# Two FFN blocks share one PSUM group for their down products, and VectorE makes all weight combinations and low parts

## The chip, the cores and the metric

One core of a Trainium2 chip. The time is device microseconds of one execution of the program. Before the change three runs took 2386.94, 2387.88 and 2385.5 us; their median is 2386.94 us. The profiled execution took 2381.64 us, of which its trace spans 2379.8.

## The reference, cut to what matters

Two layers; each mixes tokens and then runs a SwiGLU feed-forward network (FFN) on 1024 tokens of width 1024, with a hidden width of 2816 (22 blocks of 128). The change touches the FFN alone:

```python
h = modulate(rms_norm(x, g_ffn[l]), sh2, sc2)
f = (jax.nn.silu(h @ w_ffn_gate[l]) * (h @ w_ffn_up[l])) @ w_ffn_down[l]
x = x + gt2[:, None, :] * f
```

All of it is fp32. The layer's six modulation vectors come from `mod = c_act @ w_ada[l] + b_ada[l]`; those of the second layer are computed, as a side job, while the first layer's FFN runs.

## The kernel before

**Products in three parts.** A fp32 operand is split in two: a high part (rounded to fp32r, made by ScalarE) and a low part (the rest, a subtraction). A product is then three matmuls, high*high, high*low, low*high (`mm3`). "Low part" below means that subtraction.

**Blocks and jobs.** The FFN runs over 22 blocks f of 128 hidden columns. Blocks 0 and 1 are done first, in the plain way (`e_job`: 16 jobs of 12 matmuls). For f = 2 to 21 the gate and up products are made by a scheme that needs seven half-size products in place of eight: seven jobs a block (`p_job`, in the order 1, 5, 6, 2, 7, 3, 4), each of 12 matmuls into one of PSUM banks 4 to 7. Four of the seven take a sum or difference of weight halves (`comb`: q = u1 + u2, q = q - g1, u1 = g1 - u1, q = g2 - q). Then each job's weights are split: the high part on ScalarE (L1339), the low part on VectorE or GpSimd by the table `LO_ENG` (L1340). Before the change GpSimd makes all combinations (L1324) and three of seven low parts. A job's weights are prepared three jobs ahead (`look = 3`, four slots in the ring `PR`); the raw weights of the next block are loaded (`raw_load`, L1259) once job 4 has split the last of this block's.

**After a job.** `after` (L1360) adds the banks up on VectorE: seven additions out of PSUM a block, two multiplications, two SiLU on ScalarE. The block's result a (128 hidden columns x 1024 tokens) is split by `a_split` into the tile `A`: its right half after job 3, its left half after job 4, the block's last.

**Down products.** A block's down product has eight output pieces m. For each, `down_pair` does two groups (one for each half of the tokens) of three matmuls into two of PSUM banks 0 to 3, and one VectorE instruction of 128x1024 (`stt`, L204) adds the pair, times a gate, to x. They are put between the jobs by `hook`, which is called after each half job (six matmuls), 14 times a block: during block f, hooks 2 to 6 and 8 to 10 (`PAIRS`) carry the down pairs of block f - 1. So block f - 1's `A` is needed 18 matmuls after that block's last job. The down weights come through one raw buffer in halves (`dw_load`, `dw_split`) into the tile `DW`.

**Order.** TensorE runs the matmuls exactly in the order written. The other engines' orders are set by a scheduler when the program is built; each engine then works through its own list and stops at the first instruction whose operands aren't there. During the first layer's FFN `half_steps` (L1474) adds one piece of the second layer's modulation per half step: a 256 KB load, then one VectorE reduction (L1482).

**Ends.** The last two blocks' down products (20 and 21) stand in `down_tail` after the loop.

Of the kernel before, what the change touches and what calls it, by code (L numbers as in the profile page):

```python
# [17 lines left out]
HALF = 512  # L18
# [57 lines left out]
FIRST = 2  # L76
LO_ENG = {1: 0, 5: 1, 6: 0, 2: 1, 7: 0, 3: 1, 4: 0}
P_ORDER = (1, 5, 6, 2, 7, 3, 4)
PAIRS = {2: 0, 3: 1, 4: 2, 5: 3, 6: 4, 8: 5, 9: 6, 10: 7}
LATE = 11  # L80
# [51 lines left out]
class Trunk:  # L132
# [21 lines left out]

    def open(self, name, **tiles):
        cm = self.tc.tile_pool(name=name, bufs=1)
        pool = cm.__enter__()
        for nm, (n, dt) in tiles.items():
            setattr(self, nm, pool.tile([P, n], dt, name=f"{name}_{nm}"))
        return cm  # L160
# [1001 lines left out]
    def w_out(self, l):  # L1162
# [9 lines left out]
        self.hp = self.open(f"hx{l}", HX=(12 * U, F32R))  # L1172
        self.pp = self.open(f"prep{l}", FA2=(4 * U, F32))
        self.ap = self.open(f"kept{l}", FA1=(4 * U, F32))
# [125 lines left out]
    def e_hook(self, l, i):  # L1300
        if i == 0:
            self.dw_load(l, 0, 0)
        elif i == 2:
            self.shut(self.ap)
            self.ap = self.open(f"ffa{l}", A=(2 * U, F32R), DW=(2 * U, F32R))
            self.dw_split(0, 0)
            self.dw_load(l, 0, 1)
        elif i == 3:
            for half in range(2):
                self.e_split(0, half)  # L1310
            self.free.append(self.ea[0, 0])
        if i >= 4:
            self.down_pair(l, 0, i - 4)
        if i == 4:
            self.dw_split(0, 1)
            self.dw_load(l, 1, 0)
        elif i == 7:
            self.dw_split(1, 0)
            self.dw_load(l, 1, 1)

    def p_job(self, l, f, p):
        nc = self.nc
        g1, g2, u1, u2, q = [self.f(o, HALF) for o in (8 * U, 8 * U + HALF, 9 * U, 9 * U + HALF, 14 * U + HALF)]
        comb = lambda out, a, b, op=ALU.subtract: nc.gpsimd.tensor_tensor(out=out, in0=a, in1=b, op=op)  # L1324
        operand = {1: 0, 2: 1, 5: 2, 6: 3, 7: 4, 3: 5, 4: 6}[p]

        def load():
            o = self.PR()
            src = {1: g1, 5: q, 6: q, 2: g2, 7: u1, 3: q, 4: u2}[p]
            if p == 5:  # L1330
                comb(q, u1, u2, ALU.add)
            elif p == 6:
                comb(q, q, g1)
            elif p == 7:
                comb(u1, g1, u1)
            elif p == 3:
                comb(q, g2, q)
            hi, lo = self.RA[:, o:o + HALF], self.RA[:, o + HALF:o + U]
            self.act(hi, src, AF.Copy)  # L1339
            (nc.gpsimd if LO_ENG[p] else nc.vector).tensor_tensor(out=lo, in0=src, in1=hi.bitcast(F32),  # L1340
                                                                  op=ALU.subtract)
            if p == 4 and f + 1 < NRUN:
                self.raw_load(l, f + 1, "wg", 8 * U)
                self.raw_load(l, f + 1, "wu", 9 * U)
            return hi, lo
# [55 lines left out]
    def ad(self, f):  # L1401
        return (self.HX[:, :2 * U], self.HX[:, 2 * U:4 * U]) if f == NRUN - 1 else (self.A[:, :], self.DW[:, :])

# [18 lines left out]
    def down_pair(self, l, f, m):  # L1422
        d = self.fd()
        for j, n in enumerate(NS):
            self.down(f, m, n, self.bank(d + j), True, True)
        x = self.f(self.X0 + m * U, U).rearrange("p (a b) -> p a b", a=2)
        self.stt(x, self.PS[:, d:d + 2, :], self.f(self.mod[l] + 40 + m, 1), x, ALU.mult, ALU.add)

    def hook(self, l, f):
# [4 lines left out]
        if f == FIRST:  # L1434
            if i < 4:
                self.down_pair(l, 0, 4 + i)
            if i == 3:
                self.dw_split(1, 1)
                for half in range(2):
                    self.e_split(1, half)  # L1440
                self.free.append(self.ea[1, 0])
                self.dw_load(l, f, 0)
            m = i - 4
            prev = 1
        else:
            m = PAIRS.get(i, -1)
            prev = f - 1
            if i == 0:
                self.dw_load(l, f, 0)
        if f == NRUN - 1:  # L1450
            if i == 4:
                self.dw_split(f, 0)
                self.dw_load(l, f, 1)
            elif i == 6:
                self.dw_split(f, 1)
            return
        if 0 <= m < 8:
            self.down_pair(l, prev, m)
            if m == 3:
                self.dw_split(f, 0)  # L1460
                self.dw_load(l, f, 1)
            if m == 7:
                self.dw_split(f, 1)
        if self.late and i >= LATE:
            self.late()
            self.late = None
# [49 lines left out]
    def ffn(self, l, nb):  # L1516
# [29 lines left out]
        if not end:  # L1546
            ts = [self.fp(8 + k) for k in range(8)]
            na = self.norm(l + 1, 0, A, banks[0], ts, TUNE["ht_a"])
# [172 lines left out]
```

## Time and profile before

| | |
|---|---|
| runs | 2386.94, 2387.88, 2385.5 us |
| profiled execution | 2381.64 us |
| span of its trace | 2379.8 us |
| TensorE (PE) busy | 2235.3 us, 94% |
| weight loads (PEld) busy | 1793.7 us |
| VectorE (DVE) busy | 1863.8 us, 78% |
| ScalarE (ACT) busy | 967.1 us, 41% |
| GpSimd (POOL) busy | 765.8 us, 32% |

The FFN is the better part of the span: the first layer's lies at about 510 to 1200 us, the second's at 1670 to 2340 us. In a row of a timeline the first number is the start, the second how long the row lasts, and a bracket at the end says how long the engine was idle before it and what ended the idleness. Rows of several equal instructions are merged (xN). Starts of consecutive instructions on one engine can be closer than the length of one, since an instruction's end overlaps the next one's start. TensorE's matmuls have modelled ends, so the idle time of its weight loads (PEld, one for each matmul) tells more of its waits than that of the matmuls.

### The profile page before, as it was taken

How to read it: one execution, taken by the hardware profiler on the slowest of the kernel's cores; microseconds unless marked ns; L12 is line 12 of the kernel's file. 1: busy time of each engine (PE TensorE's matmuls, PEld its weight loads, DVE VectorE, ACT ScalarE, POOL GpSimd, SP SyncE). 2: the span in 40 equal slices, each digit the busy share in tenths (PEclk: the TensorE clock that was granted, in tenths of full speed). 3: DMA queues.
4: the chain of work that ended last, by engine and by line, in shares of the span. 5: the costliest groups of instructions: out<-in, count | busy, mean ns of one | idle time of the engine just before them, and what ended most of it. 6: DMA issues, size and time to landing. Idle time of an engine off the chain costs nothing.

```text
span 2379.8 us, 27251 instructions
## 1 busy us (share of the span) xinstructions
PE 2235.3 (94%) x9802; PEld 1793.7 (75%) x9802; DVE 1863.8 (78%) x2709; ACT 967.1 (41%) x1598; POOL 765.8 (32%) x559
## 2 busy tenths in 40 slices
PE   6987998999999999999989989899999999999996
PEld 4765876777777777788867777678778888888885
DVE  8888788788888888887775676987877777777775
ACT  5375475543222222222344746745422222222234
POOL 4224366202233333333200325740123323333333
PEclk9997999989999999999999999999999999999998
DMA  7323423321333333321221132323011111111112
GB/s 294 101 69 110 138 76 120 121 94 40 97 111 111 111 103 114 107 80 54 80 98 57 40 110 66 110 75 115 27 58 54 54 53 49 49 50 53 54 49 71
DMA packets 77422, 203.81 MB, mean 86 GB/s; under 512 B 8931, under 2 KB 13027, under 8 KB 77286
## 3 DMA queue, kind: packets, MB, share of 16 engines
q1 hardware_dynamic: 73540, 183.41, 23.7%
q10 hardware_dynamic: 3746, 18.66, 2.3%
q8 instruction: 77, 1.26, 0.2%
q14 instruction: 59, 0.48, 0.1%
HBM read 193.64 MB, written 8.39 MB: 85 GB/s over the span
## 4 chain that ended last, share of the span: by engine, by line
PE 72%; DVE 17%; issue 4%; ACT 4%; POOL 2%; DMA 2%; SPq 0%; POOLq 0%; ACTq 0%; DVEq 0%
PE psum L190 72%; DVE rounded L201 3%; DVE plain L201 2%; DVE plain L204 1%; DVE ffa_A L201 1%; DVE psum L885 1%; ACT rounded L198 1%; DMA plain<-in_ada 1%; ACT plain L198 1%; ACT lru_LF L198 1%; DVE psum L201 1%; DVE prep_FA L204 1%; DVE plain L312 1%; ACT ffa_A L198 1%; POOL plain L1582 1%
## 5 line engine op out<-in xcount | busy, mean ns | idle before, releaser
L190 PE MATMUL psum<-rounded 128*128 128x512 f32 (+2 forms) x4332 | 1055.4, 392 | 28.9 <-DVE rounded L201 10.2
L190 PEld LDWEIGHTS psum<-rounded 128*128 128x128 f32 (+1 forms) x4332 | 814.3, 190 | 204.3 <-DVE rounded L201 14.1
L204 DVE SCALAR_TENSOR_TENSOR plain<-psum,plain 128x1024 f32<-128x1024 f32 (+2 forms) x416 | 474.4, 1147 | 198.3 <-PE psum L190 195.8
L198 ACT ACTIVATE rounded<-plain 128x512 fp32r<-128x512 f32 (+4 forms) x412 | 272.5, 666 | 736.5 <-PE psum L190 643.3
L190 PE MATMUL psum<-ffa_A,ffa_DW 128*128 128x512 f32 (+1 forms) x2040 | 526.3, 392 | 15.6 <-DVE ffa_A L201 6.9
L190 PEld LDWEIGHTS psum<-ffa_A,ffa_DW 128*128 128x128 f32 x2040 | 379.0, 189 | 112.1 <-DVE ffa_A L201 16.3
L1324 POOL TENSOR_TENSOR plain<-plain 128x512 f32<-128x512 f32 x160 | 224.3, 1402 | 740.3 <-DMA plain<-in_wu 355.9
L190 PE MATMUL psum<-hx_HX,rounded 128*128 128x512 f32 x1488 | 381.6, 393 | 0.0
L190 PEld LDWEIGHTS psum<-hx_HX,rounded 128*128 128x128 f32 x1488 | 279.7, 188 | 61.7
L1340 POOL TENSOR_TENSOR rounded<-plain,rounded 128x512 fp32r<-128x512 f32 x120 | 173.0, 1442 | 287.4 <-ACT rounded L198 287.4
L201 DVE TENSOR_TENSOR plain<-psum,plain 128x512 f32<-128x512 f32 (+1 forms) x288 | 193.7, 686 | 25.7 <-PE psum L190 18.4
L201 DVE TENSOR_TENSOR rounded<-plain,rounded 128x512 fp32r<-128x512 f32 (+4 forms) x147 | 154.2, 1063 | 51.4 <-ACT rounded L198 48.7
L922 POOL TENSOR_TENSOR rounded<-qk_PE,rounded 128x512 fp32r<-128x512 f32 (+3 forms) x132 | 140.6, 1071 | 126.9 <-ACT rounded L198 103.8
L198 ACT ACTIVATE plain<-plain 128x512 f32<-128x512 f32 (+5 forms) x173 | 107.6, 630 | 90.7 <-DVE plain L201 53.0
L190 PE MATMUL psum<-rounded,v_V 128*65 128x512 f32 (+4 forms) x528 | 129.1, 359 | 14.6 <-ACT rounded L198 4.9
L201 DVE TENSOR_TENSOR plain<-plain 128x512 f32<-128x512 f32 (+5 forms) x156 | 133.4, 857 | 7.0 <-ACT plain L198 1.9
L190 PE MATMUL psum<-qk_QT 128*128 128x512 f32 (+8 forms) x432 | 108.3, 350 | 21.1 <-DVE plain L885 15.4
L1340 DVE TENSOR_TENSOR rounded<-plain,rounded 128x512 fp32r<-128x512 f32 x160 | 116.1, 726 | 5.6 <-ACT rounded L198 5.6
L190 PEld LDWEIGHTS psum<-rounded,v_V 128*65 128x65 f32 (+1 forms) x528 | 74.3, 150 | 53.0 <-POOL rounded L922 6.3
L201 DVE TENSOR_TENSOR psum<-psum,plain 128x256 f32<-128x256 f32 x240 | 97.7, 410 | 20.8 <-PE psum L190 13.8
L198 ACT ACTIVATE ffa_DW<-plain 128x512 fp32r<-128x512 f32 x84 | 53.0, 631 | 140.6 <-PE psum L190 138.7
L198 ACT ACTIVATE qk_PE<-psum 128x512 f32<-128x512 f32 (+4 forms) x168 | 83.3, 502 | 56.0 <-DVE psum L201 50.1
(126 smaller groups left out, 2053.3 us busy)
## 6 DMA issues: line engine op xcount, KB each, us to landing
plain<-in_ada SPq DMA_DIRECT2D x96, 256.0 KB, 2.6
plain<-in_wd SPq DMA_DIRECT2D x88, 256.0 KB, 2.6
plain<-in_wg SPq DMA_DIRECT2D x40, 512.0 KB, 3.5
plain<-in_wu SPq DMA_DIRECT2D x40, 512.0 KB, 3.7
plain<-in_ada SPq DMA_DIRECT2D x30, 512.0 KB, 3.4
start_AT<-in_ada SPq DMA_DIRECT2D x18, 512.0 KB, 5.8
plain<-in_bias_t ACTq DMA_DIRECT2D x12, 768.0 KB, 4.7
plain<-in_bias_s ACTq DMA_DIRECT2D x12, 736.0 KB, 4.2
```

Source lines behind the costliest of these rows:

```text
L190: self.nc.tensor.matmul(out=out, lhsT=lhsT, rhs=rhs, start=start, stop=stop)
L198: self.nc.scalar.activation(out=out, in_=in_, func=func, **kw)
L201: self.nc.vector.tensor_tensor(out=out, in0=a, in1=b, op=op)
L204: self.nc.vector.scalar_tensor_tensor(out=out, in0=a, scalar=s, in1=b, op0=op0, op1=op1)
L312: self.nc.vector.tensor_tensor_reduce(out=raw, in0=raw, in1=self.f(self.M0, U), op0=ALU.mult, op1=ALU.add, scale=1.0, scalar=0.0, accum_ou ...
L885: self.nc.vector.tensor_tensor_reduce(out=s, in0=s, in1=self.f(bo, a * w).rearrange("p (a b) -> p a b", a=a), op0=ALU.add, op1=ALU.max, sc ...
L922: (self.nc.vector if PLAN[self.l]["lo"][self.step] else self.nc.gpsimd).tensor_tensor(out=pl, in0=p, in1=ph.bitcast(F32), op=ALU.subtract)
L1324: comb = lambda out, a, b, op=ALU.subtract: nc.gpsimd.tensor_tensor(out=out, in0=a, in1=b, op=op)
L1340: (nc.gpsimd if LO_ENG[p] else nc.vector).tensor_tensor(out=lo, in0=src, in1=hi.bitcast(F32), op=ALU.subtract)
L1582: self.nc.gpsimd.tensor_tensor(out=x, in0=x, in1=accs[0], op=ALU.mult)
```

## The change

`A` and `DW` become two pairs of tiles: `A0`, `DW0` for even blocks, `A1`, `DW1` for odd ones. `down_pair` makes one PSUM group of six matmuls over two blocks, and one `stt` for both. The down pairs of blocks f - 2 and f - 1 stand in the hooks of the even block f (hooks 3 to 10, at f = 2 hooks 4 to 11); odd blocks carry none. The loads and splits of down weights move to match: one split in an even block, three in the odd one. `comb` goes to VectorE, and all seven low parts go to VectorE through `split`. The second pair of tiles takes the place of a scratch tile on the right side of SBUF; the norm after the first layer's FFN gets a scratch tile of its own there.

```diff
-LO_ENG = {1: 0, 5: 1, 6: 0, 2: 1, 7: 0, 3: 1, 4: 0}
-PAIRS = {2: 0, 3: 1, 4: 2, 5: 3, 6: 4, 8: 5, 9: 6, 10: 7}
+PAIRS = {i + 3: i for i in range(8)}, {i + 4: i for i in range(8)}
...
-            self.ap = self.open(f"ffa{l}", A=(2 * U, F32R), DW=(2 * U, F32R))
+            self.ap = self.open(f"ffa{l}", A0=(2 * U, F32R), DW0=(2 * U, F32R))
...
-        if i >= 4:
-            self.down_pair(l, 0, i - 4)
-        if i == 4:
+        elif i == 4:
             self.dw_split(0, 1)
             self.dw_load(l, 1, 0)
-        elif i == 7:
-            self.dw_split(1, 0)
-            self.dw_load(l, 1, 1)
...
-        comb = lambda out, a, b, op=ALU.subtract: nc.gpsimd.tensor_tensor(out=out, in0=a, in1=b, op=op)
+        comb = lambda out, a, b, op=ALU.subtract: self.tt(out, a, b, op)
...
-            self.act(hi, src, AF.Copy)
-            (nc.gpsimd if LO_ENG[p] else nc.vector).tensor_tensor(out=lo, in0=src, in1=hi.bitcast(F32),
-                                                                  op=ALU.subtract)
+            self.split(src, hi, lo)
...
     def ad(self, f):
-        return (self.HX[:, :2 * U], self.HX[:, 2 * U:4 * U]) if f == NRUN - 1 else (self.A[:, :], self.DW[:, :])
+        if f == NRUN - 1:
+            return self.HX[:, :2 * U], self.HX[:, 2 * U:4 * U]
+        return (self.A1, self.DW1) if f % 2 else (self.A0, self.DW0)
...
     def down_pair(self, l, f, m):
         d = self.fd()
         for j, n in enumerate(NS):
-            self.down(f, m, n, self.bank(d + j), True, True)
+            for i in range(2):
+                self.down(f + i, m, n, self.bank(d + j), not i, i == 1)
...
         if f == FIRST:
-            if i < 4:
-                self.down_pair(l, 0, 4 + i)
-            if i == 3:
-                self.dw_split(1, 1)
+            if i == 0:
+                self.shut(self.pp)
+                self.pp = self.open(f"ffb{l}", "right", A1=(2 * U, F32R), DW1=(2 * U, F32R))
+                self.dw_split(1, 0)
+                self.dw_load(l, 1, 1)
+            elif i == 1:
                 for half in range(2):
                     self.e_split(1, half)
                 self.free.append(self.ea[1, 0])
+            elif i == 2:
+                self.dw_split(1, 1)
                 self.dw_load(l, f, 0)
...
-        if 0 <= m < 8:
-            self.down_pair(l, prev, m)
+        m = -1 if f % 2 else PAIRS[f == FIRST].get(i, -1)
+        if m >= 0:
+            self.down_pair(l, f - 2, m)
             if m == 3:
                 self.dw_split(f, 0)
-                self.dw_load(l, f, 1)
-            if m == 7:
-                self.dw_split(f, 1)
-        if self.late and i >= LATE:
+                self.dw_load(l, f + 1 if f + 1 < NRUN - 1 else f, f + 1 == NRUN - 1)
+        if f % 2 and f < NRUN - 1:
+            if i in (1, 5, 9):
+                self.dw_split(f - (i == 5), i > 1)
+                if i < 9:
+                    self.dw_load(l, f - (i == 1), 1)
...
```

The number of matmuls does not change. How the instructions move, at the two places that matter below:

TensorE around the first down product of a block, first layer, before: `rounded` and `hx` are the seven-product jobs, `ffa` (tiles `A`, `DW`) the down products.

```order
L190 MATMUL psum<-hx_HX,rounded 128x512 x6
L190 MATMUL psum<-rounded 128x512 x24
L190 MATMUL psum<-hx_HX,rounded 128x512 x6
L190 MATMUL psum<-ffa_A,ffa_DW 128x512 x6
L190 MATMUL psum<-hx_HX,rounded 128x512 x6
L190 MATMUL psum<-ffa_A,ffa_DW 128x512 x6
```

and of the changed kernel, from the end of the even block's hooks through the odd block to the next even block's first down product (`ffa` even block, `ffb` odd block; the numbers behind them belong to the tiles' names):

```order
L189 MATMUL psum<-ffb_A_3673,ffb_DW_3674 128x512 x3
L189 MATMUL psum<-rounded 128x512 x24
L189 MATMUL psum<-hx_HX,rounded 128x512 x12
L189 MATMUL psum<-rounded 128x512 x24
L189 MATMUL psum<-hx_HX,rounded 128x512 x24
L189 MATMUL psum<-rounded 128x512 x24
L189 MATMUL psum<-hx_HX,rounded 128x512 x12
L189 MATMUL psum<-ffa_A_3599,ffa_DW_3600 128x512 x3
L189 MATMUL psum<-ffb_A_3673,ffb_DW_3674 128x512 x3
L189 MATMUL psum<-ffa_A_3599,ffa_DW_3600 128x512 x3
```

Of the last x24 (job 4 of the odd block, then job 1 of the even one) 12 matmuls follow the odd block's end, then 12 of job 5, then three for the even block's half: the odd block's `A` is needed 27 matmuls after its last job, where it was 18.

VectorE from a block's last multiplications to the low part of its left half (`ffa_A` last), first layer, before; L1482 is a modulation reduction in two rows:

```order
L1340 TENSOR_TENSOR rounded<-plain,rounded 128x512
L201 TENSOR_TENSOR plain<-plain 128x512
L201 TENSOR_TENSOR plain<-psum,plain 128x512
L201 TENSOR_TENSOR ffa_A<-plain,ffa_A 128x512
L201 TENSOR_TENSOR plain<-plain 128x512
L1482 ISA plain<-plain 128x512
L1482 ISA plain 128x1
L201 TENSOR_TENSOR ffa_A<-plain,ffa_A 128x512
```

and in the changed kernel, at the end of an odd block (`rounded` rows are low parts of weights; of the two `plain` rows merged at the top one is a combination):

```order
L200 TENSOR_TENSOR plain<-plain 128x512 x2
L200 TENSOR_TENSOR rounded<-plain,rounded 128x512
L1481 ISA plain<-plain 128x512
L1481 ISA plain 128x1
L200 TENSOR_TENSOR ffb_A_3673<-plain,ffb_A_3673 128x512
L200 TENSOR_TENSOR plain<-psum,plain 128x512
L200 TENSOR_TENSOR rounded<-plain,rounded 128x512
L200 TENSOR_TENSOR plain<-plain 128x512
L200 TENSOR_TENSOR rounded<-plain,rounded 128x512
L1481 ISA plain<-plain 128x512
L1481 ISA plain 128x1
L200 TENSOR_TENSOR ffb_A_3673<-plain,ffb_A_3673 128x512
```

Between the last addition out of PSUM and the last low part there now stand two more low parts of weights.

## Rows read from the trace of the kernel before

**Rows 1.** Windows view: stretch; busy us (xcount) of each engine, clock, DMA share, GB/s.

```profile
640.00:1016.00 376.00, 368.82 (x1582) 296.21 (x1581) 323.37 (x481) 102.04 (x168) 123.36 (x85) 1.00 0.35 110
1742.00:2283.00 541.00, 541.00 (x2362) 442.35 (x2361) 408.05 (x450) 154.14 (x251) 171.59 (x125) 1.00 0.17 53
```

**Rows 2.** Timeline of SyncE's queue: loads of raw gate weights, one a block.

```profile
640.74 0.33 SPq L1259 DMA_DIRECT2D plain<-in_wg  x1
...
1016.19 0.33 SPq L1259 DMA_DIRECT2D plain<-in_wg  x1
...
1765.69 0.33 SPq L1259 DMA_DIRECT2D plain<-in_wg  x1
...
2280.30 0.33 SPq L1259 DMA_DIRECT2D plain<-in_wg  x1
```

**Rows 3.** Waits of the weight loads, 640:1020 us: total, times, longest.

```profile
PEld psum L190 <- ACT ffa_A L198: 10.3, 13, 2.1
PEld psum L190 <- DVE ffa_A L201: 7.0, 13, 0.6
```

**Rows 4.** The same, 548:640 us (first layer, blocks 0 to 2).

```profile
PEld psum L190 <- DVE ffa_A L201: 2.7, 2, 1.7
PEld psum L190 <- ACT rounded L198: 2.0, 1, 2.0
PEld psum L190 <- DVE plain L204: 0.4, 1, 0.4
```

**Rows 5.** The same, 1708:1745 us (second layer, blocks 0 to 2).

```profile
PEld psum L190 <- DVE ffa_A L201: 2.8, 2, 1.7
PEld psum L190 <- ACT rounded L198: 2.1, 1, 2.1
```

**Rows 6.** The same, 1745:2290 us (second layer, blocks 3 to 20).

```profile
PEld psum L190 <- DVE ffa_A L201: 3.0, 17, 0.2
```

**Rows 7.** Timeline, first layer, around the end of a block at 794 us.

```profile
793.53 0.69 DVE L201 TENSOR_TENSOR plain<-plain 128x512 f32<-128x512 f32 x1
...
794.13 0.69 DVE L201 TENSOR_TENSOR plain<-psum,plain 128x512 f32<-128x512 f32 x1
...
795.04 0.88 DVE L201 TENSOR_TENSOR ffa_A<-plain,ffa_A 128x512 fp32r<-128x512 f32 x1 [0.23 <-ACT ffa_A L198]
795.34 1.73 POOL L1340 TENSOR_TENSOR rounded<-plain,rounded 128x512 fp32r<-128x512 f32 x1
795.85 1.77 DVE L201 TENSOR_TENSOR plain<-plain 128x512 f32<-128x512 f32 x1
...
797.54 0.68 DVE L1482 CUSTOM_DVE_ANT_0 plain<-plain 128x512 f32<-128x512 f32 x1
...
798.32 0.69 DVE L201 TENSOR_TENSOR ffa_A<-plain,ffa_A 128x512 fp32r<-128x512 f32 x1
798.34 0.19 PEld L190 LDWEIGHTS psum<-ffa_A,ffa_DW 128*128 128x128 f32 x1 [0.67 <-ACT ffa_A L198]
...
799.06 1.01 PEld L190 LDWEIGHTS psum<-ffa_A,ffa_DW 128*128 128x128 f32 x5 [0.54 <-DVE ffa_A L201]
```

**Rows 8.** Groups by line, whole span: count, busy us, mean ns, idle before.

```profile
L204 DVE SCALAR_TENSOR_TENSOR plain<-psum,plain 128x1024 f32<-128x1024 f32 x320 | 409.2, 1281 | 184.7 <-PE psum L190 182.4
...
L1324 POOL TENSOR_TENSOR plain<-plain 128x512 f32<-128x512 f32 x160 | 224.3, 1402 | 740.3 <-DMA plain<-in_wu 355.9 <-DVE ffa_A L201 208.1 <-DVE rounded L1340 142.6
...
L1340 POOL TENSOR_TENSOR rounded<-plain,rounded 128x512 fp32r<-128x512 f32 x120 | 173.0, 1442 | 287.4 <-ACT rounded L198 287.4
```

**Rows 9.** DMA issues on the page: count, KB each, us to landing.

```profile
plain<-in_ada SPq DMA_DIRECT2D x96, 256.0 KB, 2.6
...
plain<-in_wu SPq DMA_DIRECT2D x40, 512.0 KB, 3.7
```

**Rows 10.** Waits, whole span: GpSimd's combinations for the up weights.

```profile
POOL plain L1324 <- DMA plain<-in_wu: 355.9, 35, 12.9
```

More of the change, by code (lines that the diff above doesn't have):

```diff
@@ L152, in __init__, with open @@
         self.queue, self.look, self.sq = deque(), 1, {}
-    def open(self, name, **tiles):
-        cm = self.tc.tile_pool(name=name, bufs=1)
+    def open(self, name, side="left", **tiles):
+        cm = self.tc.tile_pool(name=name, bufs=1, side=side)
         pool = cm.__enter__()
@@ L1172, in w_out @@
         self.hp = self.open(f"hx{l}", HX=(12 * U, F32R))
-        self.pp = self.open(f"prep{l}", FA2=(4 * U, F32))
+        self.pp = self.open(f"prep{l}", "right", FA2=(4 * U, F32))
         self.ap = self.open(f"kept{l}", FA1=(4 * U, F32))
@@ L1311, in e_hook @@
             self.free.append(self.ea[0, 0])
-        if i >= 4:
-            self.down_pair(l, 0, i - 4)
-        if i == 4:
+        elif i == 4:
             self.dw_split(0, 1)
             self.dw_load(l, 1, 0)
-        elif i == 7:
-            self.dw_split(1, 0)
-            self.dw_load(l, 1, 1)
     def p_job(self, l, f, p):
-        nc = self.nc
         g1, g2, u1, u2, q = [self.f(o, HALF) for o in (8 * U, 8 * U + HALF, 9 * U, 9 * U + HALF, 14 * U + HALF)]
-        comb = lambda out, a, b, op=ALU.subtract: nc.gpsimd.tensor_tensor(out=out, in0=a, in1=b, op=op)
+        comb = lambda out, a, b, op=ALU.subtract: self.tt(out, a, b, op)
         operand = {1: 0, 2: 1, 5: 2, 6: 3, 7: 4, 3: 5, 4: 6}[p]
@@ L1441, in hook @@
                 self.free.append(self.ea[1, 0])
+            elif i == 2:
+                self.dw_split(1, 1)
                 self.dw_load(l, f, 0)
[L1443 to L1447, printed above, removed]
+        elif f % 2 == 0:
             if i == 0:
                 self.dw_load(l, f, 0)
-        if f == NRUN - 1:
-            if i == 4:
-                self.dw_split(f, 0)
-                self.dw_load(l, f, 1)
-            elif i == 6:
-                self.dw_split(f, 1)
-            return
-        if 0 <= m < 8:
-            self.down_pair(l, prev, m)
+        m = -1 if f % 2 else PAIRS[f == FIRST].get(i, -1)
+        if m >= 0:
+            self.down_pair(l, f - 2, m)
             if m == 3:
                 self.dw_split(f, 0)
-                self.dw_load(l, f, 1)
-            if m == 7:
-                self.dw_split(f, 1)
-        if self.late and i >= LATE:
+                self.dw_load(l, f + 1 if f + 1 < NRUN - 1 else f, f + 1 == NRUN - 1)
[4 more added lines that the diff above has]
+                    self.dw_load(l, f - (i == 1), 1)
+        if f == NRUN - 1:
+            if i == 1:
+                self.dw_split(f - 1, 1)
+                self.dw_load(l, f, 0)
+            elif i in (4, 7):
+                self.dw_split(f, i == 7)
+                if i == 4:
+                    self.dw_load(l, f, 1)
+        elif self.late and i >= LATE:
             self.late()
@@ L1546, in ffn @@
         if not end:
-            ts = [self.fp(8 + k) for k in range(8)]
+            self.shut(self.pp)
+            self.pp = self.open(f"tiles{l}", "right", TS=(4 * U, F32))
+            ts = [self.TS[:, k * HALF:(k + 1) * HALF] for k in range(8)]
             na = self.norm(l + 1, 0, A, banks[0], ts, TUNE["ht_a"])
```

## The prediction

> **What bounds the kernel now.** I read the windows view first. In the second layer's FFN TensorE is busy 541.00 of 541.00 us at clock 1.00; in the first layer's it is busy 368.82 of 376.00 [rows 1]. So TensorE bounds both, and a change that leaves the number of matmuls alone can only give back the time in which TensorE waits. VectorE is at 323.37 of 376.00 us (86%) in the first layer and 408.05 of 541.00 (75%) in the second [rows 1]: it bounds nothing over a stretch, but it may be late at a point. Next come the loads of gate weights, one a block. In the first layer, while the modulation side job runs, 12 blocks lie between 640.74 and 1016.19: 31.29 us a block. In the second, 17 lie between 1765.69 and 2280.30: 30.27 [rows 2]. Both have 132 matmuls a block, so one matmul costs 30.27 / 132 = 0.229 us, and a block of the first layer loses 1.02 us more than one of the second. Third, the waits of the weight loads: between 640 and 1020 us there are 13 waits for ScalarE and 13 for VectorE, all for `ffa_A`, 10.3 + 7.0 us [rows 3]. The timeline shows one pair: the first down product's first weight load comes 0.67 us late and its second 0.54 us late, the second when VectorE has made the low part [rows 7]. That is the block's own result, which the down product of the block just finished needs 18 matmuls after that block's last job (18 x 0.229 = 4.1 us).
>
> **What can be had.** In the first layer 17.3 us [rows 3]: the first of the 13 is the longest (2.1 + 0.6), the other twelve are (17.3 - 2.7) / 12 = 1.2 us each. The second layer has 3.0 us in 17 waits of at most 0.2 [rows 6], 0.18 a block. The periods check this: 1.02 + 0.18 = 1.2. At four blocks of the first layer after the side job I put 4 x 0.18 = 0.7 (estimate from [rows 6]). The start of each FFN, where the down products of blocks 0 and 1 follow hard on their making, loses 2.7 + 2.0 + 0.4 = 5.1 us [rows 4] and 2.8 + 2.1 us [rows 5] with the same 0.4 again, 5.3. Sum: 17.3 + 0.7 + 3.0 + 5.1 + 5.3 = 31.4 us. Part of each recorded wait is a short gap that would be there in any case; I take 30 (estimate: 1.4 us off for some 55 waits).
>
> **The change part by part.**
>
> Down products later. A pair of blocks now has one point where a fresh result is needed, in place of two, and it stands 24 matmuls behind the odd block's last job, plus three for the even block's half: 27 x 0.229 = 6.2 us for the high part, one matmul more, 6.4, for the low one. Before, the chain from the last addition to the end of the low part took from 794.13 to 798.32 + 0.69 = 799.01: 4.9 us [rows 7]. It holds a multiplication of 1.77 us beside a GpSimd instruction (795.34, 1.73 us); the same multiplication without one took 0.69 (793.53) [rows 7]. So with no GpSimd work there, 1.1 us goes. What comes in are two low parts of weights, which stand in VectorE's list between the last addition and the last low part. VectorE's instructions start 0.60 us apart when nothing is waited for (793.53 to 794.13 [rows 7]), so: addition, low part, multiplication, low part, reduction, five starts of 0.60 and the end of a 0.69, 3.7 us. The reduction is one in VectorE's list too, at 0.61.
>
> Is VectorE in time there? An odd block has 84 matmuls and no down products: 84 x 0.229 = 19.2 us. In VectorE's list of the first layer I count 23 instructions of 512 columns, five reductions and two tiny ones between the last additions of an even and an odd block: 23 x 0.60 + 5 x 0.61 + 0.3 = 17.2 us. That fits, with 2 us to spare. Followed through by hand: job 4's weights are split once job 6 ends (a ring slot's release, 11.0 us before the odd block's end), high part, then low part, done 9.4 us before the end; the load of the next up weights then takes 3.7 us [rows 9] and lands 5.7 us before the end; the combination q = u1 + u2 stands in VectorE's list at about -6.8, so VectorE waits 1 us there; from there on it works without a gap and starts the last addition 1.8 us after the block's end, not at 0.25. Then 3.7 us: ready at 5.6, where 6.4 is wanted. 0.8 us to spare in the first layer. In the second, without reductions, the last addition starts on time and the low part is ready at about 4, with more than 2 us to spare. So the waits at the odd blocks go; for those pairs of the first layer (seven run beside the side job) where the load is late I charge 0.2 us each, 1.4.
>
> One `stt` for two blocks. 160 of the 320 instructions of 1281 ns [rows 8] go: 205 us less of VectorE. In place of them come 160 combinations and 120 low parts, which cost GpSimd 224.3 and 173.0 us [rows 8], and VectorE 280 x 0.60 = 168. VectorE's sum falls by 37 us, plus what the GpSimd instructions cost it beside them. Since no stretch is VectorE's, this is worth nothing by itself; it is what pays for the point above. If it weren't paid, seven more instructions a block, 4.2 us, would come on 323.37 / 12 = 26.9 us a block [rows 1], 31.1 in all, and the first layer would be VectorE's.
>
> The Trainium skill, Perfetto Trace Analysis, "Optimizing Scalar/DVE Operations", speaks against the direction: with VectorE saturated, moving work from it to ScalarE or even GpSimd may make sense, though VectorE and GpSimd share a read port, so that it might not help. Here the work goes the other way, to an engine at 86%; by that rule alone the odd blocks of the first layer would be VectorE's. By the rows it is 17.2 of 19.2 us; the first rival below is that case.
>
> Combinations on VectorE. This adds a wait. On GpSimd the combination q = u1 + u2 waited 355.9 us in 35 times for the up weights, 10.2 each [rows 10], and nobody was behind it. On VectorE the same instruction holds up the additions behind it, which free PSUM banks, and through them the end of the block. At the even blocks' end it stands after the third down pair; an even block has 180 x 0.229 = 41 us for some 28 us of work (23 x 0.60 + 8 x 1.20 + 8 x 0.61). At the odd blocks' end I count 1 us, above. Bounds: 0 (landed by then) to 3.7 + 2.6 us (its own landing behind one modulation piece [rows 9]), in each of 18 pairs. I take 1, which the count gives.
>
> The FFN's start. The down products of blocks 0 and 1 move behind block 2's hook 4, 30 matmuls (6.9 us) after the second block's end. VectorE's list there has, from the product of silu and up to the low part of block 1, ten instructions, 6.3 us after a start at about 0.9: ready at 7.2, wanted 34 matmuls, 7.8 us, after. In exchange TensorE reaches the jobs of block 2 24 matmuls (5.5 us) earlier; their first weights are in VectorE's list before that with 1.5 us or more to spare. Between 0 and 1 us may be left at each start; I take 0.3 each, 0.6.
>
> Down weights. Each is loaded and split once as before; the splits of a pair stand one in the even and three in the odd block, all counted in the 23 or in the even block's slack. The sync queue has the same transfers. The tail after the loop has the same products in the same order. 0, and 0 +- 1 for the scratch tile of the next norm.
>
> **Sum.** 30 - 1.4 - 0.6 = 28 us. Span 2379.8 - 28 = 2351.8; the profiled execution, 1.8 more, 2353.6. The median of the runs lies 5.3 us above the profiled execution (2386.94 against 2381.64), so 2386.9 - 28 = 2359 us.
>
> **Rivals.**
>
> The odd blocks become VectorE's in the first layer. For it: by their lengths (0.69, a reduction 0.77) and not their starts, the 23 and the five are 19.7 us, over 19.2; the spare at the critical point is only 0.8 us; ScalarE's high parts stand between. Against: rows in the trace start 0.60 apart. Then the wait at the first down product stays, 1.2 us or more, at seven to ten pairs, and a start keeps 1 us: 28 - 12 = 16 us gained, 2371.
>
> The load holds VectorE, and the kernel is slower. If the load of the up weights lands 6.3 us behind the split that lets it start while the combination stands right behind that split, VectorE stands still for most of that. Up to 2 us are spare work time and 0.8 are spare at the down product, so each of 18 pairs loses 6.3 - 2.8 = 3.5 us: 63 us against 28 gained, 2387 + 35 = 2422. It decides from a hold of 2.8 + 28 / 18 = 4.4 us. For it: 10.2 us of waiting a block before. Against: that wait began when GpSimd had nothing else; in VectorE's new list six instructions and a reduction stand between the split and the combination, and the load has 4 us for its 3.7.
>
> The waits have another owner. If the down product waits not for the chain but for down weights or banks, half of the waits stay, since there are half as many points: 2387 - 14 = 2373. The names in [rows 3] speak against it; at the FFN's start one of three waits is for something else (2.0 us, ScalarE's `rounded` [rows 4]).
>
> **How the numbers follow.** The forecast (24 to 31 us gained) 0.70; VectorE's odd blocks or another owner (10 to 24 gained) 0.17; these with more pairs hit, so that the sum is within 0.2% (4.8 us, about what a measurement of this kernel tells from no change) 0.05; gains between 5 and 10 us 0.03; slower by the load or by VectorE 0.05. Faster by over 0.2%: 0.70 + 0.17 + 0.03 = 0.90. Range: 2355 (all of 31.4 and nothing left) to 2372 (VectorE's odd blocks).
>
> **What would show it.** The waits of the weight loads for `ffa_A` and `ffb_A` fall from 31 us to a few. Loads of gate weights come every 60.5 us for two blocks in both layers, close together at the odd block's end. VectorE's busy share in the first layer stays near 85%, and its waits for `in_wu` are about 1 us each. GpSimd is empty in the FFN. VectorE's multiplications take 0.69 us. Wrong would be: waits of jobs for the low parts of their weights (`rounded`), or for additions (`plain`), which were absent before; or a wait for `in_wu` of over 4 us on VectorE.

## The result, and the profile after

The changed kernel takes 2355.72 us (median of four runs, 2354.46 to 2356.47); the kernel before, in the same session, 2387.41 (2385.5 to 2389.18). The ratio is 0.9873, 95% interval 0.9859 to 0.9886: 31.7 us faster. The profiled executions lie 2381.64 - 2354.46 = 27.2 us apart, their spans 2379.8 - 2352.6 = 27.2.

The windows view of the changed kernel, over the stretches of [rows 1]: us; busy us (count) of TensorE, weight loads, VectorE, ScalarE, GpSimd; granted clock, DMA share, GB/s.

```profile
640.00:1016.00 376.00, 376.00 (x1646) 308.61 (x1645) 305.50 (x536) 103.94 (x172) 0.00 (x0) 1.00 0.36 112
1742.00:2283.00 541.00, 541.00 (x2367) 443.96 (x2366) 364.02 (x501) 149.33 (x249) 0.00 (x0) 1.00 0.17 51
```

TensorE is now busy all of the first layer's stretch, where it was 368.82. VectorE makes 536 instructions there in 305.50 us, before 481 in 323.37: more instructions, less time.

SyncE's queue, loads of gate weights, which answer to [rows 2]; the first and the last of six in the first layer, one a pair of blocks, and of nine in the second.

```profile
661.60 0.33 SPq L1258 DMA_DIRECT2D plain<-in_wg  x1
...
963.57 0.33 SPq L1258 DMA_DIRECT2D plain<-in_wg  x1
...
1758.36 0.33 SPq L1258 DMA_DIRECT2D plain<-in_wg  x1
...
2241.49 0.33 SPq L1258 DMA_DIRECT2D plain<-in_wg  x1
```

Five pairs in 301.97 us and eight in 483.13: 60.39 us a pair in both, which is 264 matmuls at 0.229. The side job no longer costs the first layer anything.

Waits of the weight loads for a block's own result, 548:640 and 1680:1730 us, which answer to [rows 4, 5]; for [rows 3, 6] there is no row left.

```profile
PEld psum L189 <- DVE ffb_A L200: 1.7, 2, 0.9
...
PEld psum L189 <- DVE ffb_A L200: 0.9, 1, 0.9
```

So 2.6 us of waiting remain: 0.9 at each FFN's start, and the rest at the first layer's next pair.

Timeline of the changed kernel at an odd block's end, answering to [rows 7].

```profile
798.82 0.68 DVE L200 TENSOR_TENSOR plain<-psum,plain 128x512 f32<-128x512 f32 x1
799.42 0.68 DVE L200 TENSOR_TENSOR ffb_A<-plain,ffb_A 128x512 fp32r<-128x512 f32 x1
800.02 0.68 DVE L200 TENSOR_TENSOR plain<-plain 128x512 f32<-128x512 f32 x1
800.62 0.68 DVE L1481 CUSTOM_DVE_ANT_0 plain<-plain 128x512 f32<-128x512 f32 x1
801.24 0.69 DVE L200 TENSOR_TENSOR rounded<-plain,rounded 128x512 fp32r<-128x512 f32 x1
801.84 0.68 DVE L200 TENSOR_TENSOR ffb_A<-plain,ffb_A 128x512 fp32r<-128x512 f32 x1
...
804.36 0.65 PEld L189 LDWEIGHTS psum<-ffb_A,ffb_DW 128*128 128x128 f32 x3
```

The chain from the last addition out of PSUM to the end of the last low part takes 802.52 - 798.82 = 3.7 us, where it took 4.9. TensorE's second load of the odd block's result, the first that needs the low part, comes at 804.59: 2.1 us to spare. The last addition starts 0.4 us behind the odd block's end here. In blocks 3, 5 and 7 of this FFN it starts later, 3.2, 2.1 and 1.8 us behind, and in all other odd blocks from 9 on, and in the second FFN, 0.4 to 0.8; the chain is 3.3 to 3.7 us throughout.

Groups by line and form, and VectorE's waits for the up weights, answering to [rows 8, 10].

```profile
L203 DVE SCALAR_TENSOR_TENSOR plain<-psum,plain 128x1024 f32<-128x1024 f32 x160 | 205.0, 1281 | 121.6 <-PE psum L189 120.2
...
DVE plain L200 <- DMA plain<-in_wu: 37.3, 38, 1.9
```

**Where the time came from.** In all kernels here TensorE's first 2000 matmuls are the same, and so are numbers 4651 to 6701, between the two FFNs. So the FFNs can be timed apart: from the start of matmul 2001 to that of 4651, and of 6701 to 9501. The first FFN took 627.0 us before and takes 607.7, the second 648.8 and 643.6: 19.3 + 5.2 = 24.5 us. The other 2.7 of the spans' 27.2 lie where nothing was changed: matmul 2001 starts at 533.3 us before and at 528.8 after (4.5 us less, at a mean granted clock of 0.94 and 0.95), and behind it 1.8 us go again. Over all profiles of this study matmul 2001 starts between 528.8 and 536.0.

### The profile page after: what moved, and what is told of

Its sections match the earlier page's. It is cut to its first block, busy times and chain, and to the rows that moved or that the text cites. A ratio compares the mean times of both kernels' runs of the same rounds, so it can differ in the third digit from the quotient of the medians.

```text
span 2352.6 us, 26895 instructions
## 1 busy us (share of the span) xinstructions
PE 2219.5 (94%) x9802; PEld 1789.9 (76%) x9802; DVE 1766.7 (75%) x2829; ACT 964.4 (41%) x1598; POOL 369.0 (16%) x279
## 4 chain that ended last, share of the span: by engine, by line
PE 75%; DVE 16%; issue 3%; ACT 3%; DMA 2%; POOL 1%; POOLq 0%; SPq 0%; ACTq 0%; DVEq 0%
PE psum L189 75%; DVE rounded L200 3%; DVE plain L203 1%; DVE psum L884 1%; DVE plain L200 1%; ACT lru_LF L197 1%; DVE psum L200 1%; DVE plain L311 1%; ACT plain L197 1%; POOL plain L1583 1%; DVE rounded L203 1%; DVE lru_LF L692 1%; DVE start_AT L311 1%; DMA plain<-in_ada 1%; DVE lru_LF L203 1%
## 5 line engine op out<-in xcount | busy, mean ns | idle before, releaser
L189 PE MATMUL psum<-rounded 128*128 128x512 f32 (+2 forms) x4332 | 1043.3, 391 | 29.8 <-DVE rounded L200 10.6
L200 DVE TENSOR_TENSOR rounded<-plain,rounded 128x512 fp32r<-128x512 f32 (+4 forms) x427 | 346.9, 817 | 98.4 <-ACT rounded L197 95.8
L203 DVE SCALAR_TENSOR_TENSOR plain<-psum,plain 128x1024 f32<-128x1024 f32 (+2 forms) x256 | 270.3, 1064 | 137.4 <-PE psum L189 135.8
L189 PE MATMUL psum<-hx_HX,rounded 128*128 128x512 f32 x1488 | 364.8, 392 | 0.0
L189 PE MATMUL psum<-ffa_A,ffa_DW 128*128 128x512 f32 (+1 forms) x1080 | 301.1, 389 | 0.7 <-ACT plain L197 0.7
L189 PE MATMUL psum<-ffb_A,ffb_DW 128*128 128x512 f32 x960 | 271.4, 390 | 1.3 <-DVE ffb_A L200 1.3
L189 PEld LDWEIGHTS psum<-ffa_A,ffa_DW 128*128 128x128 f32 x1080 | 202.2, 190 | 43.9 <-ACT plain L197 1.5
L200 DVE TENSOR_TENSOR plain<-plain 128x512 f32<-128x512 f32 (+5 forms) x316 | 190.6, 613 | 44.4 <-DMA plain<-in_wu 37.3
L189 PEld LDWEIGHTS psum<-ffb_A,ffb_DW 128*128 128x128 f32 x960 | 179.9, 188 | 42.4 <-DVE ffb_A L200 2.6
L197 ACT ACTIVATE ffa_DW<-plain 128x512 fp32r<-128x512 f32 x44 | 27.8, 632 | 200.4 <-PE psum L189 198.5
```

What stands on the lines that cost most here:

```text
L189: self.nc.tensor.matmul(out=out, lhsT=lhsT, rhs=rhs, start=start, stop=stop)
L197: self.nc.scalar.activation(out=out, in_=in_, func=func, **kw)
L200: self.nc.vector.tensor_tensor(out=out, in0=a, in1=b, op=op)
L203: self.nc.vector.scalar_tensor_tensor(out=out, in0=a, scalar=s, in1=b, op0=op0, op1=op1)
```

## The experiments

Gains by trace (the two FFNs, against the profile before) and by medians (against the kernel before in the same session, whose median lay between 2383.63 and 2387.41 us), us. Kernels of two sessions are compared by these gains, not by their times:

| kernel | first FFN | second FFN | sum | medians | ratio, 95% interval |
|---|---|---|---|---|---|
| changed | 19.3 | 5.2 | 24.5 | 31.7 | 0.9873 (0.9859 to 0.9886) |
| e1 pairs alone | -19.0 | 0.3 | -18.7 | -13.1 | 1.0051 (1.0035 to 1.0067) |
| e2 VectorE alone | 2.4 | -7.1 | -4.7 | -1.5 | 0.9998 (0.9987 to 1.0009) |
| e3 later hooks alone | 4.2 | 0.3 | 4.4 | 6.2 | 0.9968 (0.9955 to 0.9981) |
| e10 VectorE + later hooks, no pairs | 17.7 | 3.0 | 20.8 | 21.9 | 0.9902 (0.9886 to 0.9919) |
| e9 changed, additions twice | 17.0 | 3.7 | 20.7 | 25.4 | 0.9886 (0.9866 to 0.9905) |
| e5 pairs, combinations on VectorE | 10.0 | 3.1 | 13.2 | 17.6 | 0.9928 (0.9909 to 0.9946) |
| e6 pairs, low parts on VectorE | -8.8 | 0.0 | -8.7 | -0.8 | 1.0002 (0.9990 to 1.0014) |
| e4 changed, pairs two hooks earlier | -1.7 | 0.5 | -1.1 | 0.0 | 0.9996 (0.9985 to 1.0007) |
| e7 changed, pairs one hook later | 19.5 | 6.2 | 25.7 | 31.1 | 0.9866 (0.9849 to 0.9883) |
| e8 changed, up weights loaded twice | 12.3 | 5.3 | 17.5 | 21.2 | 0.9904 (0.9888 to 0.9920) |

The theory was the prediction's: the later need removes the wait, and VectorE's work is what pays for it and what endangers it. Its rivals: another owner of the wait, VectorE as the bound, and any one part of the change doing all of it.

**e1: pairs alone**, with combinations and three low parts on GpSimd as before.

```diff
+LO_ENG = {1: 0, 5: 1, 6: 0, 2: 1, 7: 0, 3: 1, 4: 0}
...
-        comb = lambda out, a, b, op=ALU.subtract: self.tt(out, a, b, op)
+        comb = lambda out, a, b, op=ALU.subtract: nc.gpsimd.tensor_tensor(out=out, in0=a, in1=b, op=op)
...
-            self.split(src, hi, lo)
+            self.act(hi, src, AF.Copy)
+            (nc.gpsimd if LO_ENG[p] else nc.vector).tensor_tensor(out=lo, in0=src, in1=hi.bitcast(F32),
+                                                                  op=ALU.subtract)
```

> The pairing alone: the changed kernel with the combinations and three of seven low parts put back on GpSimd. Theory (the gain comes from where the fresh result is needed, 27 matmuls or 6.2 us after the block in place of 18 or 4.1 us): the chain keeps its 4.9 us beside GpSimd, still under 6.2, so nearly all goes as in the full change: gain 24 to 28 us, waits of the weight loads for ffa and ffb under 4 us, about 2359 to 2363. Rival A (VectorE needs the GpSimd work gone to be in time): half of the points wait as before, gain 14, about 2373. Rival B (the gain is that of the shorter VectorE chain): gain under 6.

It was slower: 2398.12 us (before 2384.98), which neither the theory nor rival A had. Waits of the weight loads in the first FFN (528:1182 us), then ScalarE's for combinations over the whole span, in e1 and in the kernel before:

```profile
PEld psum L190 <- ACT ffb_A L198: 21.3, 8, 3.8
PEld psum L190 <- DVE ffb_A L201: 6.1, 10, 1.5
...
ACT rounded L198 <- POOL plain L1319: 115.2, 40, 3.8
...
ACT rounded L198 <- POOL plain L1324: 53.1, 19, 3.5
```

and its timeline at the end of an odd block:

```profile
822.29 0.68 DVE L201 TENSOR_TENSOR plain<-psum,plain 128x512 f32<-128x512 f32 x1
822.31 1.29 POOL L1335 TENSOR_TENSOR rounded<-plain,rounded 128x512 fp32r<-128x512 f32 x1
823.68 1.28 POOL L1319 TENSOR_TENSOR plain<-plain 128x512 f32<-128x512 f32 x1
824.99 0.64 ACT L198 ACTIVATE rounded<-plain 128x512 fp32r<-128x512 f32 x1 [3.68 <-POOL plain L1319]
825.53 0.61 ACT L198 ACTIVATE plain<-plain 128x512 f32<-128x512 f32 x1
...
831.72 0.63 ACT L198 ACTIVATE ffb_A<-plain 128x512 fp32r<-128x512 f32 x1 [3.58 <-DVE plain L201]
...
832.41 0.19 PEld L190 LDWEIGHTS psum<-ffb_A,ffb_DW 128*128 128x128 f32 x1 [2.79 <-ACT ffb_A L198]
```

GpSimd's combination follows its low part, 1.3 us a link (one instruction of the chain of combinations and low parts); ScalarE's high part stands 3.68 us behind it, and the `silu` at 825.53, whose input VectorE had added up by 822.97, stands in order behind that; with it the block's result is late. The odd block has 19.2 us for the chain of GpSimd that had 30 before. The longest waits are also followed by a lower granted clock. Windows of e1, columns as above, around another odd block's end, where a wait of 3.3 us for the block's result ends 0.7 us into the second stretch; the last line is the sum over seven windows, one at each place of the first FFN where the clock fell (573:580, 638:645, 768:771, 833:836, 897:904, 966:969, 1031:1034):

```profile
885.00:897.00 12.00, 9.89 (x44) 7.75 (x42) 9.11 (x15) 2.95 (x5) 8.30 (x6) 1.00 0.19 53
897.00:904.00 7.00, 6.29 (x14) 4.71 (x15) 4.07 (x8) 2.15 (x4) 1.27 (x1) 0.53 0.38 138
904.00:911.00 7.00, 7.00 (x31) 5.70 (x31) 4.15 (x8) 0.64 (x1) 0.00 (x0) 0.98 0.21 63
...
sum 33.00, PE 29.82 PEld 22.66 DVE 19.94 ACT 7.34 POOL 8.15; mean PE 4.26 PEld 3.24 DVE 2.85 ACT 1.05 POOL 1.16
```

14 matmuls in 6.29 us busy at clock 0.53 (near the 1.2 GHz level), 0.45 us each; 31 in the 7.00 after, 0.23 each. Over 540 to 1180 us the clock is 0.97, where it is 1.00 before and after the change. This is the larger part of what e1 loses in the first FFN. Its waits in the first FFN come to about 28 us, where the kernel before has 23 in the same FFN, only 5 less. The 73 matmuls of the seven windows took 29.82 us; at 0.229 each they would have taken 16.7, so the clock cost some 13 us (an estimate from these rows). Together that is 18 of the 19.0 us. The profiled execution is the longest of e1's six (2392.22 to 2404.73 us).

**e2: VectorE alone**: the kernel before with `comb` through `self.tt` and all low parts on VectorE.

```diff
-LO_ENG = {1: 0, 5: 1, 6: 0, 2: 1, 7: 0, 3: 1, 4: 0}
+LO_ENG = {1: 0, 5: 0, 6: 0, 2: 0, 7: 0, 3: 0, 4: 0}
...
-        comb = lambda out, a, b, op=ALU.subtract: nc.gpsimd.tensor_tensor(out=out, in0=a, in1=b, op=op)
+        comb = lambda out, a, b, op=ALU.subtract: self.tt(out, a, b, op)
```

> The other half alone: the kernel before, with all combinations and low parts on VectorE, down products as before. Theory: seven more VectorE instructions a block (4.2 us) on 26.9 of 31.3 us in the first layer, less some 1.3 us that GpSimd's instructions cost it there: 29.8 us of work against 30.2 us of matmuls, so VectorE is late at more points; the chain of 4.9 us loses 1.1 and gains 1.2. The waits for ffa stay or grow: 1.2 us a block in the first layer becomes 2 to 4, the second layer has 25.7 of 30.2 us and 0.2 to 1 a block: 10 to 45 us slower, about 2405. Rival (taking the work off GpSimd helps by itself, since VectorE's multiplications fall from 1.8 to 0.7 us): 5 to 15 us faster, about 2377.

2386.52 us: no change, and not slower as expected. By the traces it is two things: the first FFN gains 2.4 us and the second loses 7.1. Waits of the weight loads, 640:1020 and then 1740:2290 us:

```profile
PEld psum L190 <- DVE ffa_A L201: 10.8, 13, 1.0
PEld psum L190 <- ACT ffa_A L198: 2.0, 3, 0.8
...
PEld psum L190 <- DVE ffa_A L201: 11.2, 18, 0.6
```

About 1.0 us a block in the first layer and 0.6 in the second: the chain ends that much behind the 18 matmuls (in the second layer it was 0.2 before [rows 6]). Both are below 1.4 us, the six matmuls between two hooks.

**e3: later hooks alone**: the kernel before, down products one hook later.

```diff
-PAIRS = {2: 0, 3: 1, 4: 2, 5: 3, 6: 4, 8: 5, 9: 6, 10: 7}
+PAIRS = {3: 0, 4: 1, 5: 2, 6: 3, 7: 4, 8: 5, 9: 6, 10: 7}
```

> The kernel before with one table changed: the eight down pairs of a block stand at hooks 3 to 10 in place of 2 to 6 and 8 to 10, so the result is needed 24 matmuls (5.5 us) after its block, not 18 (4.1 us). Theory: 5.5 is over the chain's 4.9, so the waits of blocks 3 to 20 go (17.3 + 0.7 + 3.0 us recorded), the starts of the FFN keep theirs (10.4): gain 17 to 21, about 2368. Rival (fewer points and the VectorE time saved are what counts; one hook later only moves the wait): gain under 6, about 2383.

2378.75 us. The second layer's waits went but for one at the FFN's start, the first layer's did not. Waits in 640:1020, then in 1740:2290 us, then the window view:

```profile
PEld psum L190 <- DVE ffa_A L201: 7.0, 13, 0.5
PEld psum L190 <- DVE plain L204: 5.2, 12, 1.0
PEld psum L190 <- ACT ffa_A L198: 1.4, 4, 0.5
...
PEld psum L190 <- DVE ffa_A L201: 1.7, 1, 1.7
...
640.00:1016.00 376.00, 372.41 (x1600) 298.39 (x1599) 329.65 (x487) 102.31 (x170) 130.22 (x86) 1.00 0.36 111
```

A new wait took the place of half of the old one: TensorE waits for banks (`plain L204`), since VectorE is behind.

**e10: both, without pairs**: the edits of e2 and e3 together.

> The kernel before, without pairs, with its down products one hook later (hooks 3 to 10) and all combinations and low parts on VectorE. It tells whether the pairs are needed beside a later need and short links. Theory: they are; 320 additions leave VectorE some 31 us of work a block of the first layer, so it stands behind at each block's end, and TensorE waits for banks and for the result: 2375 to 2390 us. Rival: the need moved 2.7 us and links of 0.60 us are enough, and pairing adds nothing: 2356 to 2362.

(The six matmuls between hooks are 1.4 us, not 2.7 as written there and for e7.) 2361.74 us: at the upper end of the rival's range, and my theory, that pairs are needed, fell; that pairing adds nothing does not follow (below). Its windows and waits (540:640, and the same at the second FFN's start; none in 640:1020):

```profile
640.00:1016.00 376.00, 376.00 (x1643) 308.07 (x1642) 359.28 (x583) 104.48 (x174) 0.00 (x0) 1.00 0.37 115
...
PEld psum L190 <- DVE ffa_A L201: 2.5, 2, 1.4
```

VectorE is busy 359.28 of 376 us (96%) and TensorE does not wait for it in that stretch. The groups of the multiplications and combinations of 512 columns, 625:985 us, in e3:

```profile
L201 DVE TENSOR_TENSOR plain<-plain 128x512 f32<-128x512 f32 x23 | 28.7, 1247 | 0.0
```

and in e10:

```profile
L201 DVE TENSOR_TENSOR plain<-plain 128x512 f32<-128x512 f32 x71 | 47.1, 683 | 0.0
```

With GpSimd at work one takes 1247 ns, without it 683. e3 and e10 differ in nothing but the engine of the combinations and low parts. VectorE makes 96 instructions more in the stretch (583 against 487) for 29.6 us more (359.28 against 329.65), 0.31 us each, where one takes 0.60 by itself. Whether e3 lags because VectorE's instructions are longer or because of GpSimd's own links was not separated.

**e9: additions twice**: the changed kernel with the line of `down_pair` that calls `self.stt` written twice.

> The changed kernel with each of its 160 additions over 1024 columns made twice (the product is added a second time), so that VectorE has as many of them as the kernel before. It tests the step that the halving pays for the 280 instructions that came from GpSimd. Theory (the prediction's: unpaid, VectorE needs 31.1 us a block and the first layer is VectorE's): eight times 1.28 us more a pair of blocks on 295 of 360 us gives 356 of 360 in the first layer, every list late by a block's end: 2367 us or more, with waits for banks (plain) and for the odd block's result. Rival: the additions stand in the even block, which has 41 us for 28 us of VectorE's work, and are made up by the odd block's end: 2356 to 2360.

2358.28 us: the rival. VectorE is busy 356.63 of 376 us (95%), near the theory's 99%, but TensorE's waits (640:1020) come to 3.7 us:

```profile
PEld psum L189 <- DVE ffb_A L200: 3.4, 6, 1.0
PEld psum L189 <- ACT ffb_A L197: 0.3, 1, 0.3
```

So the halved additions are worth 3.8 us by the FFNs and 6.3 by the gains of two sessions, and do not carry the gain. They do carry its spare: from 640 to 1020 us the last addition now starts 2.7 to 3.6 us behind the odd block's end, and the low part is ready 6.4 to 7.3 us behind it, where it is wanted at 6.4.

**e5 and e6: GpSimd's part taken apart.** Pairs as changed; in e5 the low parts of e1 are on GpSimd (and no `comb`), in e6 the combinations (and no low part).

> Pairs as in the changed kernel, combinations on VectorE, but the three low parts of jobs 5, 2 and 3 on GpSimd again. Theory: pairing alone lost because GpSimd could not make the chain of combinations (1.3 to 1.7 us a link, where VectorE has 0.60) within the short odd block, so ScalarE stood in order behind it. Four of its seven links are back on VectorE; what stays is that a combination that writes q has to wait until GpSimd's low part has read it. Then most of the gain is there: 2358 to 2368 us. Rival, any GpSimd link costs alike: four sevenths of the way from 2398 (pairs alone) to 2356 (the change), 2374. Second rival, GpSimd's work beside VectorE's is what costs (1.77 us against 0.69 for an addition) and VectorE now waits for GpSimd in order: no faster than before, 2385 or more.

> Pairs as in the changed kernel, all low parts on VectorE, but the four combinations on GpSimd. Theory (the combinations make the chain late): ScalarE and VectorE both stand in order behind a chain that still starts when GpSimd has the up weights and goes on at 1.3 to 1.7 us a link: 2385 to 2400 us, with waits of ScalarE for combinations near the 102.7 us of pairs alone. Rival, any GpSimd link costs alike: three sevenths of the way from 2398 to 2356, 2380. Second rival, the low parts are what matters: 2360.

2368.99 and 2387.36 us. Of the 44.8 us between the gains of pairs alone and of the changed kernel, four combinations a block on VectorE give 30.7, three low parts alone 12.3: combinations weigh more, as the theory had it. e5 came out 1 us above the theory's range and 5 below the rival's 2374. ScalarE's waits for combinations in e6 stay near e1's, and its granted clock over the first FFN is 0.98:

```profile
ACT rounded L197 <- POOL plain L1317: 99.6, 40, 3.9
```

**e4 and e7: the need moved.** `PAIRS` of the changed kernel two hooks earlier ({i + 1}; a hook is six matmuls) and one later ({i + 4}, in block 2 {i + 5}). In e7 the last of the eight pairs of blocks 0 and 1 multiplies the right half of block 2's result in place of block 0's; the instructions are the same.

> The changed kernel with the pairs of blocks f - 2 and f - 1 two hooks earlier (hooks 1 to 8 of the even block), so the odd block's result is needed 15 matmuls (3.4 us) after its block in place of 27 (6.2). In the changed kernel's trace the low part is ready 2.1 to 2.3 us ahead of need at nine pairs of the second layer, 0.4 to 2.3 at eight of the first and 0.7 late at one. Theory: 2.75 us less makes each pair late by the difference: 12 us in the first layer, 5 in the second, 14 to 18 us slower than the changed kernel, about 2372. Rival (pairing itself, with half as many points, is what removes the wait): within 4 us of the changed kernel, about 2357.

> The changed kernel with its down pairs one hook later (hooks 4 to 11, in block 2 hooks 5 to 12). Theory: the need moves 12 matmuls (2.7 us) back, so the waits left at the two starts and at the first pair behind them, 2.6 us in all, go: 2353 us, the waits for the odd block's result at nothing. Rival: the last addition over 1024 columns now comes one hook nearer to the block's end, VectorE starts the end's additions late and TensorE waits for banks, as it did in the kernel before with its hooks one later (0.4 us a block there): 2356 to 2362.

e4 took 2384.96 us: all of the gain gone, twice what was expected. Its waits, 640:1020, then the end of an odd block, whose job 4 is the first half of the x24:

```profile
PEld psum L189 <- ACT ffb_A L197: 8.3, 6, 1.6
PEld psum L189 <- DVE ffb_A L200: 5.3, 6, 1.0
...
810.97 5.65 PE L189 MATMUL psum<-rounded 128*128 128x512 f32 x24
...
815.62 0.68 DVE L200 TENSOR_TENSOR plain<-psum,plain 128x512 f32<-128x512 f32 x1
...
818.63 0.69 DVE L200 TENSOR_TENSOR ffb_A<-plain,ffb_A 128x512 fp32r<-128x512 f32 x1
```

13.6 us for six pairs, 2.3 each. The position of the need does decide. The wait is longer than the 2.7 us taken away less the spare of 0.4 to 2.3 that the changed kernel has, since that spare is no longer there: the block ends at about 813.7 us, the last addition starts 1.9 us behind it (1.6 to 2.1 at the six), and the chain is still 3.7 us. Why VectorE is later there than in the changed kernel stays open. The clock takes a part too: it is 0.58 in 693:697 and 0.50 in 820:823 us. e7 took 2355.48 us: the starts' waits went, and 1.9 us came in 640:1020, 1.3 of it for banks. No gain that can be told.

**e8: up weights loaded twice** (`self.raw_load(l, f + 1, "wu", 9 * U)` written twice; the second goes when the first has landed).

> The changed kernel with each block's load of up weights issued twice into the same place, so that it lands about 3.6 us later. VectorE's wait for it, 1.0 us each in 38, becomes about 4.6 us. By the prediction's rule (2.8 us of spare a pair, break-even at a hold of 4.4 us) each of 18 pairs then loses 4.6 - 2.8 = 1.8 us: 32 us, 2388, no gain left. Theory from the changed kernel's trace: margins at the need are 1.8 to 2.3 us in most pairs, and in the second layer VectorE is 68% busy and catches up; only the first layer's pairs lose: 2362 to 2375. Rival: the two transfers run beside each other and the wait hardly grows: 2356.

2365.31 us, within the theory's range, but not by its mechanism: VectorE's wait did not grow to 4.6 us.

```profile
DVE plain L200 <- DMA plain<-in_wu: 35.4, 22, 2.3
```

VectorE's order is made when the program is built, with the load's length in view. In the changed kernel the low part of down weights follows the combination:

```profile
817.78 1.42 DVE L200 TENSOR_TENSOR plain<-plain 128x512 f32<-128x512 f32 x2 [0.80 <-DMA plain<-in_wu]
819.12 0.68 DVE L200 TENSOR_TENSOR ffa_DW<-plain,ffa_DW 128x512 fp32r<-128x512 f32 x1
```

in e8 it stands ahead, with other work:

```profile
827.88 0.69 DVE L200 TENSOR_TENSOR ffa_DW<-plain,ffa_DW 128x512 fp32r<-128x512 f32 x1 [1.27 <-ACT ffa_DW L197]
...
833.15 0.69 DVE L200 TENSOR_TENSOR plain<-plain 128x512 f32<-128x512 f32 x1 [1.58 <-DMA plain<-in_wu]
```

So the longer load made the chain later without holding the engine. The second rival's break-even, a hold of 4.4 us, is untested.

## Why the prediction was right, and where it was not

- **What can be had.** The place was right: the waits for a block's own result. The size: 31.4 us recorded, 30 taken. Of those waits 28.8 went and the two FFNs became 24.5 us shorter by the profiles: about 4 us of the recorded waits, not 1.4, gave nothing back. e3 shows where: it took the second layer's 3.0 us of waits of at most 0.2, and that FFN became 0.3 us shorter. So the agreement of the 28 us with the 27.2 between the profiled executions is in part luck: 2.7 of these lie in stages that the change does not touch. The medians give more (31.7, interval 27.2 to 33.7). The profiled execution of before lies 5.8 us under the median that the gain is counted from (2387.41), that of after 1.3 under its own; the forecast, which took the gain of one execution off the median, leaves that out. In which stage the other executions of before lose those 5 us, no profile shows.
- **The later need.** 27 matmuls in place of 18 was counted rightly, and e4 shows that it decides: with the pairs two hooks earlier the gain is gone. But pairs alone (e1) do not give it.
- **VectorE in time.** The chain was worked out at 3.7 us and is 3.7. It was expected 1.8 us late at its start with 0.8 us to spare. That is what blocks 5 and 7 of the first FFN have (2.1 and 1.8 us late, 0.4 and 0.7 to spare); block 3 is 3.2 late and costs a wait, and all later ones are 0.4 to 0.8 us late with 1.8 to 2.3 to spare. The second layer's "more than 2 us" holds (2.1 to 2.3).
- **Charges.** 1.4 + 0.6 = 2.0 us expected, 2.6 recorded, but elsewhere: 0.9 at each start (0.3 expected), 0.8 at one pair, nothing at the other six.
- **Combinations on VectorE.** A hold of 1 us was taken; 37.3 / 38 = 1.0.
- **What pays for it: wrong.** The step "if it weren't paid, 31.1 in all, and the first layer would be VectorE's" adds seven instructions at 0.60 us to 26.9 us a block. Those 26.9 us were long because GpSimd worked beside them. e10 has the seven without the halving: 359.28 / 376 x 30.2 = 28.9 us a block, and no wait there. Moving the work made VectorE's other instructions shorter by half of what it added (e3 to e10: 29.6 us for 96 instructions). So the first rival, whose case was this load, was further off than its price said, and what the halving and pairing add is the difference of e10 and the changed kernel: 3.8 us by the FFNs, 9.8 by the gains of two sessions. Of the 3.8, 2.4 are waits at the two FFNs' starts and just behind them (5.0 in e10, 2.6 in the changed kernel).
- **The cause, as the runs leave it.** The gain needs two things: the weight chain on VectorE (short links, and no GpSimd beside it; no run separates these two) and a need some 1.4 us later. Either alone gives -1.5 (e2) or 6.2 us (e3), both together 21.9 (e10). Pairs give the later need too, but shorten every odd block to 19.2 us, which GpSimd's chain can't keep up with: the waits stay as long as before in half as many places, the clock falls behind the longest of them, and pairs alone give -13.1, with VectorE's chain 31.7.

The rule weighed in the prediction (the Trainium skill, Perfetto Trace Analysis, "Optimizing Scalar/DVE Operations") is that work may be moved from a saturated VectorE even to GpSimd, though with the read port that they share it might not help. The runs bear out the reservation, seen from the other side: work taken from GpSimd cost VectorE half of its own length (e3 to e10), and at 96% busy it held TensorE up nowhere in that stretch. That the port is what had slowed VectorE, no run here shows. The changed kernel's fall from 86 to 81% (305.50 of 376.00) has the halved additions in it as well.

## What to carry to other kernels

Where two engines share one chain, count the chain's links by the shortest stretch between two points of need, not by the mean over blocks: e1 cut that stretch from 30 to 19 us and lost 13 us with less work on VectorE and no more elsewhere. Fewer waits that are longer can cost more than many short ones of the same sum, when the clock falls behind them. An in-order engine that takes one input from a slow chain passes the delay on to all that stands behind it. An engine's load after a move is not its load before plus what it takes over, where the engine that it takes it from had been slowing it.

## What the runs showed of the hardware

A VectorE instruction on 512 columns with both inputs and its output in SBUF takes 683 ns alone and 1247 ns on average with GpSimd at work (e10, e3), 1.77 us in [rows 7]; one that reads one input from PSUM took 681 ns in e10 and 680 in e3. After a wait of TensorE of 3.3 us the granted clock was 0.53 over 7 us, and 14 matmuls took 6.29 us in place of 3.2 (e1): the wait cost about twice itself. In e4 it was down to 0.58 and 0.50 in two windows, where no wait of the stretch was longer than 1.6 us; with e2's waits of at most 1.0 us it stayed at 1.00 over both stretches.
